# Token lists of a mixture-of-experts layer: half of them by scatters spread over the projections, half by one-hot products

## The chip, the cores and the metric

One core of a Trainium2 chip runs the whole kernel. The metric is the device time of one execution in microseconds (us), lower is better. TensorE (PE) multiplies matrices, VectorE (DVE) and ScalarE (ACT) work element by element, GpSimd (POOL) does some of that and issues all indirect DMAs, SyncE (SP) issues most loads. The engines run side by side, each through its own instructions in order, and wait for one another by semaphores.

## The reference

One decoder layer on 1024 tokens of width 1024, in float32: a mixer with one input and one output projection, a layer norm, a mixture of experts, and a second layer norm.

```python
proj = h @ w_in                       # 2560 columns: q, f, v, g of 4 heads, 4 pooling groups
...
h = layer_norm(ALPHA * h + mix @ w_out)
scores = sigmoid(h @ w_router)        # 64 experts
sel = scores + router_bias            # best 4 of 8 groups, then the best 8 experts in them
wts = scores[chosen] / sum * 2.5
for each expert e, for its tokens t:  # 256 hidden columns
    out[t] += wts[t, e] * (silu(h[t] @ w_gate[e]) * (h[t] @ w_up[e])) @ w_down[e]
out += shared expert on every token
return layer_norm(ALPHA * h + out)
```

Each token has 8 experts, so 8192 pairs of token and weight have to be sorted by expert before the experts can run: for each expert a list of its token numbers and a list of the weights. These lists are what the change is about.

## The kernel before, in words

The 1024 tokens are eight tiles of 128, in two halves. For each half the kernel projects x (20 projections of 128 columns, each 24 matmuls: 8 pieces of the contraction, three products each, since every operand is split into a high and a low float32r part), and after each projection it takes one to three pieces of the recurrent heads from the list `pend` (`for i, (kind, h) in enumerate(kinds[hf])`, line 854). Then `out_project(hf, ...)` does the output projection and layer norm. The one for the first half stands before the sixth projection of the second half (`OUT0_AT`).

At the end of an output projection two pairs of tiles are normed in turn, and `route(t0, pair)` is called for each pair (the second half's first pair somewhat later, among the matmuls of the next). It does four things. `choose` multiplies by the router's weights, takes the sigmoid (`scored[0]`) and finds the eight experts of a token; `mb` and `mk` are the 0/1 masks. `slots_of` counts with a triangular matrix on PE how many earlier tokens chose the same expert; that gives `code`, for each token and expert the row in a table in DRAM (`table`, 64 experts x 1152 slots x 2 numbers), and `c8`, the eight rows of each token. `send` works out the eight weights of each token on DVE (line 663) and issues, for each tile and each of its eight choices, an indirect DMA on POOL that writes 128 pairs of 8 bytes to these rows: 16 scatters for a pair of tiles, 64 in all (line 667). `preset` writes two tiles to the sums in DRAM.

After the last pair `rank_experts` sorts the experts by their load on PE and DVE (`perm` is the permutation matrix, `ids_i` the experts' numbers, by which the weights are loaded), and `send` issues the last 16 scatters. `rank_tables` reads 192 slots of each expert's list back through SP (line 737), makes three repeated copies on POOL (line 742) and turns the lists by matmuls with `perm` into `idx_a`, `idx_c`, `idx_s` and the gates: the row numbers by which POOL gathers tokens (line 904). It is called when the first routed unit is loaded, after the two units of the shared expert. Between the routing and the routed stage PE has the shared expert's work: four tiles held on the chip (`SharedHeld`, two groups: gate and up for all four, then down), and two units `Shared`. Then come 64 experts' units: gather, transposes, gate and up, down, scatter-add (line 1198), with the weights (3 MB for each expert) loaded by SP and split by ACT (line 71) and DVE (line 72).

The order of the instructions on each engine is made by a planner with cost estimates, which may move work as far as its data allow; `tc.issue_after(x)` ties instructions behind `x`. Only in the routed stage the order on PE is the one written. PSUM has four banks "pj", two "lv" and two "mi", taken in turn; a bank is taken again when its last reader is done.

Of the kernel before, what the change touches and what calls it, by code (L numbers as in the profile page):

```python
# [50 lines left out]
BEHIND = 3  # L51
IN_RANGE = "ids, counts and blocks are worked out on the chip within these bounds for any scores"
# [3 lines left out]
def tile_layer(ctx: ExitStack, tc: tile.TileContext, x, w_in, hg_lb_logits, hg_norm_g, w_pool, pool_scale, w_out,  # L56
# [385 lines left out]
    waiting = []  # L442
# [5 lines left out]
    def out_project(hf, mx, groups):  # L448

        hts = {}  # L450
        after = []
        for tiles, cols in groups:
            if cols[0] == 0:
                for t in tiles:
                    hts[t] = rows_tile()
                    r0 = (hf * NC4 + t) * P
                    nc.gpsimd.dma_start(hts[t], x[r0:r0 + P, :])
            pss = {(t, n): bank("pj") for t in tiles for n in cols}
            for i, k in enumerate(OUT_ORDER):
# [12 lines left out]
            if cols[-1] == 1:  # L472
                batches = [b for b in BATCHES[hf] if b[0] in tiles]
                for batch in batches:
                    pair = [hts[t] for t in batch]
                    layer_norm(rt, pair, lng, lnb, hf)
                    for t in batch:
                        nc.scalar.dma_start(h_ext[(hf * NC4 + t) * P:(hf * NC4 + t + 1) * P, :], hts[t])
                    go = lambda t0=hf * NC4 + batch[0], pair=pair: route(t0, pair)
                    if hf and tiles != groups[-1][0]:  # L480
                        after.append(go)
                    else:
                        chosen = go()
        return hf * NC4 + batches[-1][0], chosen

    def route(t0, pair):
        while waiting:
            with tc.issue_after(normed[0].ins):
                send(*waiting.pop())
        chosen = choose(t0, pair)  # L490
        if t0 + len(pair) < SEQ // P:
            waiting.append((t0, chosen, slots_of(t0, chosen)))
            if t0 < NC4:
                send(*waiting.pop())
        with tc.issue_after(scored[0].ins):
            preset(t0, pair)
        if t0 == NC4:
            shared_weights()
        return chosen
# [6 lines left out]
    def setup_dram(z):  # L506
        for i in range(DUMMY // P):
            nc.gpsimd.dma_start(h_ext[SEQ + i * P:SEQ + (i + 1) * P, :], z)
            nc.gpsimd.dma_start(acc[SEQ + i * P:SEQ + (i + 1) * P, :], z)
        pad = t2("k", 2).rearrange("p (s o) -> p s o", o=2)[:EXPERTS]  # L510
        nc.gpsimd.memset(pad, 0)
        nc.gpsimd.iota(pad[:, :, 0], pattern=[[1, DUMMY]], base=SEQ, channel_multiplier=0, allow_small_or_imprecise_dtypes=True)
        tv = table.rearrange("(e s) o -> e s o", s=SLOTS)
        for c in range(0, SLOTS, DUMMY):
            n = min(DUMMY, SLOTS - c)
            nc.gpsimd.dma_start(tv[:, c:c + n, :], pad[:, :n, :])
# [21 lines left out]
    def setup_router():  # L538
# [11 lines left out]
        nc.vector.tensor_scalar(tri, jp, 0.0, None, op0=ALU.is_gt)  # L550
        nc.vector.memset(onesb, 1.0)
# [4 lines left out]
    def rtile(tag, shape, dt=F32):  # L556
        if tag in places:
# [66 lines left out]
    def slots_of(t0, chosen):  # L624
# [25 lines left out]
        return code, c8, wt  # L650

    def send(t0, chosen, placed):

        hts = chosen[0]
        code, c8, wt = placed
        T = len(hts)
        pair = pairs[:, t0:t0 + T]
        scr = rtile("wscr", [EXPERTS])
        ci = slots[:, t0:t0 + T]
        placed_at[0] = nc.vector.tensor_scalar(ci, c8, -1.0, None, op0=ALU.add)  # L660
        for t in range(T):
            for j in range(8):
                nc.vector.scalar_tensor_tensor(scr[:, t, :], code[:, t, :], c8[:, t, j:j + 1], wt[:, t, :], op0=ALU.is_equal, op1=ALU.mult,
                                               accum_out=pair[:, t, j, 1:2])
        for t in range(T):
            for j in range(8):
                sc = nc.gpsimd.indirect_dma_start(out=table[:, :], out_offset=bass.IndirectOffsetOnAxis(ap=ci[:, t, j:j + 1], axis=0),
                                                  in_=pair[:, t, j, :], in_offset=None)
                for o in scatters:
                    tc.declare_no_dep(sc.ins, o.ins, reason="each token of an expert has a slot of its own")  # L670
                scatters.append(sc)
# [6 lines left out]

    ids_i = rc.tile([1, EXPERTS], I32, name="ids_i")
# [9 lines left out]
    def rank_experts(mb):  # L689
        E = EXPERTS  # L690
# [4 lines left out]
        for i, m in enumerate(parts):  # L695
            nc.tensor.matmul(pc[:E, E:E + 1], m, onesb[:, 0:1], start=i == 0, stop=m is parts[-1])
        cnt = rc.tile([P, 1], F32, name="cnt")
        nc.vector.tensor_copy(cnt[:E], pc[:E, E:E + 1])
        col = rc.tile([P, 2], F32, name="col")
        nc.gpsimd.iota(col[:, 0:1], pattern=[[0, 1]], base=0, channel_multiplier=1, allow_small_or_imprecise_dtypes=True)  # L700
        nc.vector.scalar_tensor_tensor(col[:E, 1:2], cnt[:E], float(E), col[:E, 0:1], op0=ALU.mult, op1=ALU.subtract)
# [3 lines left out]
        nc.vector.tensor_scalar(key[:E], key[:E], col[:E, 1:2], None, op0=ALU.is_gt, op1=ALU.add, accum_out=rank[:E])  # L705
        perm = rc.tile([P, E], F32, name="perm")
        nc.vector.tensor_scalar(perm[:E], iota_e[:E], rank[:E], None, op0=ALU.is_equal)
# [26 lines left out]
    def rank_tables(perm, tmp):  # L734
        E = EXPERTS
        lists = tmp[:, :384].rearrange("p (s o) -> p s o", o=2)
        nc.sync.dma_start(lists, table.rearrange("(e s) o -> e s o", s=SLOTS)[:, 0:192, :])
        p3 = bank("mi")
        nc.tensor.matmul(p3[:, 0:E], lists[:, 0:P, 0], perm[:E], start=True, stop=True)
        for i, n in enumerate((64, 32, 16)):  # L740
            same = tmp[:, 384 + i * P:512 + i * P]
            nc.gpsimd.tensor_copy(same.rearrange("p (m s) -> p m s", s=n), lists[:, None, P:P + n, 0].to_broadcast([E, P // n, n]))
            nc.tensor.matmul(p3[:, (1 + i) * E:(2 + i) * E], same, perm[:E], start=True, stop=True)
        for q in range(2):
            n = P if q == 0 else 64
            nc.tensor.matmul(p3[:n, (4 + q) * E:(5 + q) * E], lists[:, q * P:q * P + n, 1], perm[:E], start=True, stop=True)
        nc.vector.tensor_copy(idx_a, p3[:, 0:E])
# [14 lines left out]
        nc.vector.tensor_copy(gate_a, p3[:, 4 * E:5 * E])  # L762
        nc.vector.tensor_copy(gate_s, p3[0:64, 5 * E:5 * E + N_REST])
# [86 lines left out]
    for hf in range(2):  # L850
# [3 lines left out]
        for i, (kind, h) in enumerate(kinds[hf]):  # L854
            if hf == 1 and i == OUT0_AT:
                out_project(0, mx[0], GROUPS[0])
            if hf == 0 and i == 2:
# [4 lines left out]
            ps = project(kind, h, xT, lambda: pend and pend.pop(0)())  # L862
            if hf == 0 and i == 0:
# [18 lines left out]
    while pend:  # L882
        pend.pop(0)()
    left.close()
# [7 lines left out]
    t0, chosen = out_project(1, mx[1], GROUPS[1])  # L892
    right.close()
    cp = right.enter_context(tc.tile_pool(name="cp", bufs=1, side="right"))
    perm, counts = rank_experts(chosen[1])
    send(t0, chosen, slots_of(t0, chosen))
# [4 lines left out]
    lists = rt.tile([64, D], F32, tag="yc", name="yc", bufs=2)[:EXPERTS]  # L901
# [367 lines left out]
    def load_to(n):  # L1269
        while n_loaded[0] < min(n, len(units)):  # L1270
            if n_loaded[0] == n_shared:
                rank_tables(perm, lists)
# [100 lines left out]

    worst = load_i(nblk_i[0:1, EXPERTS:EXPERTS + 1], 0, MAX_BLOCKS, mybir.ALL_ENGINES)
    with tc.If(worst > 0):
        with tc.For_i(0, EXPERTS) as r:
# [71 lines left out]
```

## Time and profile before

| | |
|---|---|
| median of 3 runs | 1455.69 us (1450.94 to 1456.17) |
| the profiled execution | 1448.83 us |
| its span | 1447.1 us, mean granted PE clock 0.956 |
| busy | PE 91%, DVE 75%, ACT 60%, POOL 39% |
| DMA | 350 MB, mean 242 GB/s; 14480 packets under 512 B |

The span is the time from the first to the last instruction of the profiled execution. A busy share is that of the whole span; matmuls overlap in a pipeline, so a PE that is busy all the time need not be at its peak. The clock is that which the chip granted to PE, 1.00 for 2.4 GHz and 0.50 for 1.2 GHz. A releaser behind "<-" is what ended an engine's wait; "remote" is a signal that the profile can't put down to an instruction, and "issue" is a wait that nothing in the profile shows.

### The profile page before, as it was taken

What the parts mean: (1) busy time and instruction counts of PE and PEld (TensorE: products, weight loads), DVE (VectorE), ACT (ScalarE), POOL (GpSimd) and SP (SyncE); (2) the same over time, 40 slices, a digit from 0 to 9 for tenths busy, and PEclk for the clock granted to TensorE, in tenths of its full rate; (3) what the DMA queues carried; (4) which work ended last, traced back from release to release, by engine and by line L of the source; (5) the groups of instructions that cost most, each with busy time, mean ns of one, the idle gap of its engine ahead of it and who ended that gap; (6) DMA issues with size and microseconds to landing.
All of it is one profiled execution on the core that took longest, in us unless ns stands there. A gap on an engine that the chain in (4) does not pass through costs nothing. (4 is left out here: it accounts for less than half of the span.)

```text
span 1447.1 us, 21911 instructions
## 1 busy us (share of the span) xinstructions
PE 1323.3 (91%) x7055; PEld 1103.9 (76%) x7056; DVE 1087.4 (75%) x2168; ACT 871.6 (60%) x1625; POOL 558.3 (39%) x471
## 2 busy tenths in 40 slices
PE   8799999977998866999999899898999989999992
PEld 6688878866876655788877688787888877888871
DVE  6466864866777844777888688888889888888856
ACT  5233442332434221677777688777888877888855
POOL 3000000045012442454343455664656636565415
PEclk9899999997999988999999999999999999999996
DMA  7422243433125426999999899999999989999975
GB/s 236 153 59 66 59 126 92 134 108 73 51 74 181 140 61 201 327 352 337 322 355 349 258 364 328 319 361 336 323 365 353 344 292 330 360 352 351 365 201 219
DMA packets 138661, 350.07 MB, mean 242 GB/s; under 512 B 14480, under 2 KB 55520, under 8 KB 138544
## 3 DMA queue, kind: packets, MB, share of 16 engines
q1 hardware_dynamic: 110864, 258.08, 49.3%
q0 software_dynamic: 25664, 83.22, 22.1%
q10 hardware_dynamic: 2016, 7.34, 1.3%
q8 instruction: 56, 0.92, 0.2%
q14 instruction: 61, 0.50, 0.1%
HBM read 296.36 MB, written 52.23 MB: 241 GB/s over the span
## 5 line engine op out<-in xcount | busy, mean ns | idle before, releaser
L72 DVE TENSOR_TENSOR lo<-raw,hi 128x1024 fp32r<-128x1024 f32 (+1 forms) x490 | 485.4, 1024 | 62.6 <-ACT hi L71 50.3
L71 ACT ACTIVATE hi<-raw 128x1024 fp32r<-128x1024 f32 (+1 forms) x490 | 418.0, 888 | 49.5 <-DMA raw<-in_w_gate_dram 16.7
L1198 POOL DMA_INDIRECT acc<-ya,idx_a x64 | 149.4, 2334 | 289.7 <-ACT hi L71 77.5
L1159 PE MATMUL pj<-xt,hi 128*128 128x288 f32 (+3 forms) x768 | 205.8, 351 | 6.8 <-POOL xt L1145 4.8
L71 ACT ACTIVATE whi<-wraw 128x512 fp32r<-128x512 f32 x128 | 80.6, 630 | 205.6 <-PE pj L79 100.1
L1159 PE MATMUL pj<-xt,lo 128*128 128x144 f32 (+3 forms) x768 | 174.1, 237 | 0.0
L1159 PEld LDWEIGHTS pj<-xt,hi 128*128 128x128 f32 x768 | 150.5, 196 | 11.1 <-POOL xt L1145 5.3
L1159 PEld LDWEIGHTS pj<-xt,lo 128*128 128x128 f32 x768 | 149.8, 199 | 0.8
L78 PE MATMUL pj<-hi,xt 128*128 128x512 f32 x368 | 149.2, 406 | 0.8 <-DVE sg L1163 0.7
L79 PE MATMUL pj<-lo,xt 128*128 128x512 f32 x368 | 145.4, 395 | 0.0
L80 PE MATMUL pj<-hi,xt 128*128 128x512 f32 x368 | 145.0, 394 | 0.0
L72 DVE TENSOR_TENSOR wlo<-wraw,whi 128x512 fp32r<-128x512 f32 x112 | 76.6, 688 | 86.6 <-ACT whi L71 85.5
L78 PE MATMUL pj<-xh,whi 128*128 128x512 f32 x320 | 133.3, 417 | 2.0 <-ACT whi L71 2.0
L80 PE MATMUL pj<-xh,wlo 128*128 128x512 f32 x320 | 131.0, 410 | 0.0
L79 PE MATMUL pj<-xl,whi 128*128 128x512 f32 x320 | 130.1, 406 | 0.0
L78 PE MATMUL pj<-hi,hTh 128*128 128x512 f32 x240 | 98.1, 409 | 18.5 <-ACT hTh L71 15.9
L72 DVE TENSOR_TENSOR xt<-lv,xt 128x512 fp32r<-128x512 f32 x148 | 96.5, 682 | 11.5 <-ACT xt L71 10.8
L904 POOL DMA_INDIRECT h<-h_ext,idx_a x64 | 93.0, 1453 | 29.2 <-PE lv L916 11.4
L79 PE MATMUL pj<-lo,hTh 128*128 128x512 f32 x240 | 97.0, 404 | 0.0
L71 ACT ACTIVATE xt<-lv 128x512 fp32r<-128x512 f32 x148 | 81.7, 595 | 24.2 <-PE lv L916 15.3
L80 PE MATMUL pj<-hi,hTl 128*128 128x512 f32 x240 | 95.0, 402 | 0.0
L1193 POOL TENSOR_SCALAR yc<-yc,gate_s 16x1024 f32<-16x1024 f32 (+3 forms) x24 | 84.2, 3509 | 7.7 <-DVE yc L1192 7.7
(354 smaller groups left out, 2786.3 us busy)
## 6 DMA issues: line engine op xcount, KB each, us to landing
raw<-in_w_down_dram SPq DMA_DIRECT2D x128, 512.0 KB
raw<-in_w_gate_dram SPq DMA_DIRECT2D x127, 512.0 KB
raw<-in_w_up_dram SPq DMA_DIRECT2D x127, 512.0 KB
wraw<-in_w_in_dram SPq DMA_DIRECT2D x80, 256.0 KB
wraw<-in_w_out_dram SPq DMA_DIRECT2D x48, 256.0 KB
h<-in_x_dram POOLq DMA_DIRECT2D x8, 512.0 KB
h_ext<-h ACTq DMA_DIRECT2D x8, 512.0 KB
raw<-acc SPq DMA_DIRECT2D x8, 512.0 KB
```

The lines of the kernel that those rows point to most:

```text
L71: last_split[0] = nc.scalar.activation(hi, src, AF.Copy)
L72: (eng or nc.vector).tensor_sub(lo, src, hi.bitcast(F32))
L78: nc.tensor.matmul(ps, sh, mh, start=first, stop=False)
L79: nc.tensor.matmul(ps, sh, ml, start=False, stop=False)
L80: last_mm[0] = nc.tensor.matmul(ps, sl, mh, start=False, stop=last)
L904: nc.gpsimd.indirect_dma_start(out=g, out_offset=None, in_=h_ext[:, :], in_offset=bass.IndirectOffsetOnAxis(ap=idx, axis=0))
L1159: nc.tensor.matmul(ps[q][:, :cols], w, x[:, :cols], start=k + i == 0, stop=k + i == NK)
L1193: nc.gpsimd.tensor_scalar(rest[:cut], rest[:cut], gate_s[:cut, r:r + 1], None, op0=ALU.mult)
L1198: return nc.gpsimd.indirect_dma_start(out=acc[:, :], out_offset=bass.IndirectOffsetOnAxis(ap=idx, axis=0), in_=y, in_offset=None, compute_ ...
```

## The change

The first four tiles keep their scatters. Their routing is cut into steps that stand between the pieces of the heads in `pend`, and the 32 scatters become a list `drops`, of which three are issued after each projection, the first of the three behind the projection's last matmul. The last four tiles have no scatters. For each tile and choice, `list_up` makes a tile `sel` (for each token a row of 64 token numbers and 64 weights that is zero but at the chosen expert) and a tile `at` (for each token a row of 192 seats that is zero but at the token's seat), and adds `sel` transposed times `at` in one PSUM bank on PE: 128 rows (64 lists of numbers, 64 of weights) by 192 seats. The lists of the first half are read from the table into `kept`, and the sum of both is what `rank_tables` takes, now directly behind. Only 192 slots for each expert are cleared at the start; the whole table is filled and all 64 scatters are issued in a branch for experts with too many tokens, which is taken only for such scores.

```diff
+DROPS = 3
+LISTED = 192
...
+    def route_early(t0, pair):
+        got = []
+        def scores():
+            got.append(choose(t0, pair))
+            with tc.issue_after(scored[0].ins):
+                preset(t0, pair)
+        def places():
+            drops.extend(send(t0, slots_of(t0, got[0])))
+        return [scores, places]
...
+    def drop(n):
+        for i in range(min(n, len(drops))):
+            with tc.issue_after(last_mm[0].ins):
+                sc = drops.pop(0)()
+            if i == 0:
+                tc.add_manual_dep(sc.ins, last_mm[0].ins.name, ..., reason="a few at a time")
...
+    def list_up(t0, placed, ps, sels, first, last):
+        code, c8, wt, pos = placed
+        for t in range(2):
+            for j in range(8):
+                sel = sels[j % len(sels)]
+                at = cp.tile([P, LISTED], F32, tag="at", name="at", bufs=2)
+                gates(t0, placed, t, j, sel[:, 1])
+                nc.gpsimd.tensor_scalar(sel[:, 0], code[:, t, :], c8[:, t, j:j + 1], pairs[:, t0 + t, j, 0:1], op0=ALU.is_equal, op1=ALU.mult)
+                nc.vector.tensor_scalar(at, seats, pos[:, t, j:j + 1], None, op0=ALU.is_equal)
+                nc.tensor.matmul(ps, sel.rearrange("p a e -> p (a e)"), at, start=first and t + j == 0, stop=last and t + j == 8)
...
                 out_project(0, mx[0], GROUPS[0])
+                pend = [step for steps in itertools.zip_longest(routing, pend) for step in steps if step]
...
             ps = project(kind, h, xT, lambda: pend and pend.pop(0)())
+            drop(DROPS)
...
+    nc.gpsimd.iota(seats, pattern=[[1, LISTED]], base=SEQ, ...)
+    for q in range(2):
+        read = nc.gpsimd.dma_start(kept[q * EXPERTS:(q + 1) * EXPERTS], table.rearrange("(e s) o -> e s o", s=SLOTS)[:, 0:LISTED, :])
+        ...
+    listed = bank("pj")[:, :LISTED]
+    list_up(late[0][0], late[0][2], listed, sels, True, False)
+    perm, counts = rank_experts(late[1][1][1])
+    placed = slots_of(late[1][0], late[1][1])
+    ...
+    list_up(late[1][0], placed, listed, sels, False, True)
+    for q in range(2):
+        e = slice(q * EXPERTS, (q + 1) * EXPERTS)
+        nc.vector.tensor_add(lists[e], listed[e], kept[e, :, q])
+    rank_tables(perm)
```

`rank_tables` loses its read of the table; its three copies move from POOL to DVE. `rank_experts` counts on 128 partitions instead of 64.

## Rows read from the trace of the kernel before

**Rows 1.** Windows: engines' busy us (instructions), PE clock, DMA share, GB/s.

```profile
250.00:300.00 50.00, 50.00 (x252) 41.91 (x251) 39.18 (x104) 16.65 (x29) 1.06 (x2) 1.00 0.46 143
300.00:350.00 50.00, 36.36 (x175) 28.98 (x174) 27.40 (x161) 12.87 (x29) 33.76 (x33) 0.80 0.31 82
600.00:800.00 200.00, 200.00 (x957) 161.83 (x956) 163.18 (x210) 153.81 (x240) 87.16 (x41) 1.00 1.02 344
800.00:1400.00 600.00, 574.28 (x3382) 494.63 (x3381) 508.55 (x789) 483.92 (x935) 328.30 (x264) 0.97 0.99 333
```

**Rows 2.** The tile table: instructions, count, min/median/max ns, first and last start.

```profile
L667 POOL DMA_INDIRECT table<-pairs,slots x64: 953/963/2053, 305.0 to 552.5; - x64
L737 SPq DMA_DIRECT2D yc<-table x1: 562/562/562, 568.5 to 568.5; - x1
```

**Rows 3.** Windows: the stretches at the lower clock in the projections.

```profile
320.00:330.00 10.00, 4.01 (x18) 3.11 (x19) 3.94 (x26) 2.67 (x6) 6.43 (x8) 0.50 0.29 39
330.00:335.00 5.00, 5.00 (x23) 4.59 (x22) 5.00 (x34) 0.56 (x1) 3.91 (x4) 0.64 0.48 187
345.00:350.00 5.00, 4.87 (x12) 3.28 (x12) 1.58 (x7) 0.00 (x0) 4.00 (x4) 0.50 0.21 53
```

**Rows 4.** Timeline, POOL and ACT: start, us, instruction, idle before it, releaser.

```profile
304.96 1.10 POOL L667 DMA_INDIRECT table<-pairs,slots  x1 [16.95 <-DVE passing L663]
312.87 0.55 ACT L323 ACTIVATE sc<-lv 32x128 f32<-32x128 f32 x2 [4.64 <-remote]
329.95 1.02 POOL L667 DMA_INDIRECT table<-pairs,slots  x1 [2.35 <-DVE passing L663]
341.42 0.28 ACT L380 ACTIVATE w<-mi 128x128 f32<-128x128 f32 x1 [5.12 <-remote]
```

**Rows 5.** Windows: between the last output projection and the routed stage.

```profile
510.60:516.10 5.50, 0.37 (x2) 0.00 (x0) 0.00 (x0) 0.38 (x1) 4.28 (x5) 0.86 0.02 1
516.10:521.30 5.20, 5.17 (x15) 4.30 (x16) 0.00 (x0) 0.00 (x0) 3.00 (x4) 0.50 0.02 1
545.00:556.60 11.60, 0.14 (x2) 0.00 (x0) 2.38 (x7) 0.40 (x2) 6.68 (x7) 0.66 0.39 129
556.60:562.00 5.40, 5.36 (x13) 4.20 (x14) 2.15 (x4) 0.26 (x1) 0.00 (x0) 0.50 0.31 90
575.00:585.14 10.14, 8.64 (x45) 6.81 (x46) 8.08 (x21) 4.66 (x7) 7.53 (x7) 1.00 0.84 283
```

**Rows 6.** Timeline: the last routing and the lists, several engines.

```profile
515.69 0.38 ACT L585 ACTIVATE passing<-mi 128x256 f32<-128x256 f32 x1 [7.29 <-remote]
533.62 0.95 POOL L667 DMA_INDIRECT table<-pairs,slots  x1 [13.62 <-DVE passing L663]
552.55 0.96 POOL L667 DMA_INDIRECT table<-pairs,slots  x1 [0.30 <-issue]
556.21 0.66 ACT L71 ACTIVATE hTh<-mi 128x256 fp32r<-128x256 f32 x2 [11.99 <-remote]
577.86 0.23 DVE L747 CAST idx_a<-mi 128x64 int32<-128x64 f32 x1 [1.64 <-PE mi L746]
```

**Rows 7.** Durations: timeline once, then by line and shape: busy us, mean ns.

```profile
466.63 1.81 PE L579 MATMUL lv<-ident,h 128*128 128x128 f32 x8
L663 DVE SCALAR_TENSOR_TENSOR passing<-code,c,wt 128x64 f32<-128x64 f32 x32 | 7.0, 283 | 0.0
L72 POOL TENSOR_TENSOR wlo<-wraw,whi 128x512 fp32r<-128x512 f32 x16 | 21.6, 1359 | 109.4 <-ACT whi L71 94.6 <-DVE sc L327 14.7
L742 POOL COPY yc<-yc 64x128 f32<-64x128 f32 x3 | 1.7, 597 | 21.6 <-DMA raw<-in_w_down_dram 21.6
```

**Rows 8.** Timeline: a line of DVE beside POOL's work, and alone.

```profile
485.61 1.37 POOL L72 TENSOR_TENSOR wlo<-wraw,whi 128x512 fp32r<-128x512 f32 x1 [0.98 <-ACT whi L71]
486.22 0.80 DVE L609 TENSOR_SCALAR gr<-gr 128x16 f32<-128x16 f32 x1
526.05 0.17 DVE L609 TENSOR_SCALAR gr<-gr 128x16 f32<-128x16 f32 x1
```

More of the change, by code (lines that the diff above doesn't have):

```diff
@@ L478, in out_project, with route_late @@
                         nc.scalar.dma_start(h_ext[(hf * NC4 + t) * P:(hf * NC4 + t + 1) * P, :], hts[t])
-                    go = lambda t0=hf * NC4 + batch[0], pair=pair: route(t0, pair)
-                    if hf and tiles != groups[-1][0]:
-                        after.append(go)
-                    else:
[L483 to L489, printed above, removed]
-        chosen = choose(t0, pair)
[L491 to L496, printed above, removed]
+                    t0 = hf * NC4 + batch[0]
+                    if hf == 0:
+                        routing.extend(route_early(t0, pair))
+                    elif tiles != groups[-1][0]:
+                        after.append(lambda t0=t0, pair=pair: route_late(t0, pair))
+                    else:
+                        route_late(t0, pair)
+    routing = []
+    late = []
+    drops = []
+    def route_early(t0, pair):
[7 more added lines that the diff above has]
+        return [scores, places]
+    def route_late(t0, pair):
+        chosen = choose(t0, pair)
         if t0 == NC4:
+            late.append((t0, chosen, slots_of(t0, chosen)))
             shared_weights()
-        return chosen
+        else:
+            late.append((t0, chosen, None))
+    def drop(n):
[3 more added lines that the diff above has]
+            if i == 0:
+                tc.add_manual_dep(sc.ins, last_mm[0].ins.name, mybir.DependencyInfo(mybir.DependencyClass.Sync, mybir.DependencyReason.DATA), reason="a few at a time")
     h_ext = dram.tile([SEQ + DUMMY, D], F32, name="h_ext")
@@ L509, in setup_dram @@
             nc.gpsimd.dma_start(acc[SEQ + i * P:SEQ + (i + 1) * P, :], z)
[L510 to L516, printed above, removed]
+        nc.gpsimd.dma_start(table.rearrange("(e s) o -> e (s o)", s=SLOTS)[:, :2 * LISTED], z[:EXPERTS, :2 * LISTED])
     wr = rt.tile([P, NK * P], F32R, tag="xc", name="wr", bufs=2).rearrange("p (k e) -> p k e", k=NK)
@@ L556, in rtile @@
     def rtile(tag, shape, dt=F32):
+        if tag in ("gsc", "gr"):
+            c = places["lt"] + (0 if tag == "gsc" else 16)
+            return passing[:, c:c + 16].rearrange("p (t c) -> p t c", t=2)
         if tag in places:
@@ new lines, in slots_of, with gates @@
+        pos = rtile("pos", [8])
+        for t in range(T):
+            nc.vector.max(pos[:, t, :], base[:, t, :])
+        placed_at[0] = nc.vector.scalar_tensor_tensor(pos, c8, float(SEQ), pos, op0=ALU.add, op1=ALU.subtract)
+        return code, c8, wt, pos
+    def gates(t0, placed, t, j, out):
+        code, c8, wt, _ = placed
+        nc.vector.scalar_tensor_tensor(out, code[:, t, :], c8[:, t, j:j + 1], wt[:, t, :], op0=ALU.is_equal, op1=ALU.mult,
+                                       accum_out=pairs[:, t0 + t, j, 1:2])
@@ L658, in send @@
+    def send(t0, placed):
         scr = rtile("wscr", [EXPERTS])
-        ci = slots[:, t0:t0 + T]
-        placed_at[0] = nc.vector.tensor_scalar(ci, c8, -1.0, None, op0=ALU.add)
-        for t in range(T):
+        for t in range(2):
             for j in range(8):
-                nc.vector.scalar_tensor_tensor(scr[:, t, :], code[:, t, :], c8[:, t, j:j + 1], wt[:, t, :], op0=ALU.is_equal, op1=ALU.mult,
-                                               accum_out=pair[:, t, j, 1:2])
-        for t in range(T):
-            for j in range(8):
[L667 to L671, printed above, removed]
+                gates(t0, placed, t, j, scr[:, t, :])
+        return [lambda t=t, j=j: to_table(t, j) for t in range(t0, t0 + 2) for j in range(8)]
@@ new lines, in to_table @@
+    def to_table(t, j):
+        sc = nc.gpsimd.indirect_dma_start(out=table[:, :], out_offset=bass.IndirectOffsetOnAxis(ap=slots[:, t, j:j + 1], axis=0),
+                                          in_=pairs[:, t, j, :], in_offset=None)
+        for o in scatters:
+            tc.declare_no_dep(sc.ins, o.ins, reason="each token of an expert has a slot of its own")
+        scatters.append(sc)
+        return sc
+    def list_up(t0, placed, ps, sels, first, last):
+        code, c8, wt, pos = placed
+        for t in range(2):
+            for j in range(8):
+                sel = sels[j % len(sels)]
[4 more added lines that the diff above has]
+                nc.tensor.matmul(ps, sel.rearrange("p a e -> p (a e)"), at, start=first and t + j == 0, stop=last and t + j == 8)
@@ L694, in rank_experts @@
             nc.tensor.matmul(pc[:, 0:E], onesb, m, start=i == 0, stop=m is parts[-1])
[L695 to L701, printed above, removed]
+        for q in range(2):
+            for i, m in enumerate(parts):
+                nc.tensor.matmul(pc[q * E:(q + 1) * E, E:E + 1], m, onesb[:, 0:1], start=i == 0, stop=m is parts[-1])
+        nc.vector.tensor_copy(cnt, pc[:, E:E + 1])
+        nc.vector.scalar_tensor_tensor(col[:, 1:2], cnt, float(E), col[:, 0:1], op0=ALU.mult, op1=ALU.subtract)
         key = rc.tile([P, E], F32, name="key")
```

73 lines of the change are left out of this document (48 added, 25 removed).

## The prediction

> **What bounds the kernel now.** I read four views in this order. First the busy time by stretches: where does TensorE (PE) stand idle or run at the lower clock? From 600 to 800 us PE is busy for 200.00 of 200.00 us at clock 1.00 [rows 1]. That is the first quarter of the routed stage, so whatever makes that stage start earlier makes the kernel end earlier, as far as nothing else binds later. The projections of the first half run as well: 50.00 of 50.00 us between 250 and 300 [rows 1]. The stretch 300 to 350, which is the same kind of work, has 36.36 us and clock 0.80 [rows 1]. Something costs 13.6 us of idle time there, and a slow clock after it.
>
> Second, the view by tile of the table says what is different: 64 scatters of token lists on GpSimd (POOL), median 963 ns, the first at 305.0, the last at 552.5 [rows 2]. They come in four runs of 16, two in the projections, from 304.96 and 329.95 [rows 4], two after them. In a run one starts every 1.26 us: from 533.62 to 552.55 there are 15 steps [rows 6].
>
> Third, the timeline says how a scatter on POOL can stop PE. While a run lasts, signals between the other engines come late: ScalarE (ACT) waits 4.64 and 5.12 us, each ended by "remote", for results that PE has long issued [rows 4]. In the last run the wait is 11.99 us, and it ends at 556.21, under four microseconds after the last scatter started [rows 6]. So a scatter is not dear by itself; a long run of them is. The waits don't start with the run. The first run begins at 304.96, and the wait that ends at 312.87 began at 308.2, three scatters later; the second begins at 329.95, and the wait that ends at 341.42 began at 336.3, with its sixth scatter [rows 4]. I don't know the mechanism; I take the rows.
>
> Fourth, the end of the chain for the lists: they are read back at 568.5 [rows 2], behind the stores that the SP queue holds, and the indices for the first gather exist at 577.86 [rows 6].
>
> **The change part by part.** *Early scatters (the first four token tiles).* The same 32 scatters stay, in 11 groups of up to three after eleven projections. A group lasts 3 x 1.26 = 3.8 us; each group waits for the projection's last matmul, and behind that wait on POOL stand only the next scatters and the loads of x for the second output projection, which nothing wants before the projections are over. The routing steps are put between the head parts; from the loops I count that the list of head parts is as long at the end (5) as before, so nothing new is left over there. What the two runs cost now: idle 50 - 36.36 = 13.6 us; and work at the lower clock, 4.0 us of it between 320 and 330 at 0.50, 3.6 us between 330 and 335 (0.64 is 72% at 0.5), 4.9 us between 345 and 350 [rows 3], half of 12.5, or 6.2 us. Together 19.8 us. Ends of the gain: 19.8 if groups of three delay nothing, since no such wait began before the third scatter of its run; 0 if every scatter costs its 0.6 us wherever it stands; a loss is not excluded, one late signal per group, 11 x 0.5 us, or -5. I take 16, near the upper end, because the rows show the first three scatters of both runs free.
>
> *Late scatters (the last four tiles).* 32 scatters, the list read on SP and its landing go. What they cost on PE, by stretches [rows 5]: 510.6 to 516.1, idle 5.1; 516.1 to 521.3 at clock 0.50, 2.6 lost; 545 to 556.6, idle 11.5; 556.6 to 562 at 0.50, 2.7 lost; 575 to 585.1, idle 1.5 while lists and first gathers are waited for. Sum 23.4 us.
>
> *What is added on PE.* 32 matmuls in float32, 128 x 128 by 192 columns. Eight of 128 columns took 1.81 us [rows 7], 0.226 each; by columns 0.34, times 32 is 10.9 us. Ends: 7.2 us if a matmul costs no more than one of 128 columns, 21.7 us if all run at the lower clock.
>
> *What is added on VectorE (DVE) and POOL.* A step makes two one-hot tiles: a gate product on DVE (there before too, 0.28 us [rows 7]), a comparison of 128 x 192 on DVE (estimate 0.25 us, between 0.17 for one input of 16 columns with POOL idle [rows 8] and the 0.28) and a product on POOL of 128 x 64, between 0.597 us for a copy of 64 x 128 and 1.36 us for 128 x 512 with two inputs [rows 7]; I take 0.6. Do DVE and POOL overlap? The rows say not always: while POOL worked from 485.61 for 1.37 us, a DVE operation on 16 columns, issued at 486.22, took 0.80 us and ended with it; the same line took 0.17 us with POOL idle [rows 8]. So I let a step take the sum, 0.6 + 0.28 + 0.25 = 1.13 us, instead of 0.6. For the last pair of tiles that is 16 x 1.13 = 18.1 us where 16 scatters took 16 x 1.26 = 20.2.
>
> The Trainium skill ("SBUF — State Buffer", § SBUF: two separate sides) says that VectorE and GpSimd hold one port pair exclusively, for a whole instruction, when VectorE runs in a two-port mode or reads two inputs from SBUF. The trace agrees in the 0.80 us above. By that rule the 18.1 us stand, without it the list would be 9.6 us; it speaks against this change, since it moves a step of the lists from the DMA to exactly this pair.
>
> *When the lists are ready.* The last pair's scores waited 7.29 us for a late signal at 515.69 [rows 6]. Without scatters I put the start of the last pair's lists 7 us earlier, at 526.5 instead of 533.6. Then 18.1 for the steps and some 3 for ranking give indices at about 547.6, 30 us earlier than now. PE then has the shared expert's work for the last four tiles to do, so most of these 30 us are not on its path. One thing is: the product sums in one of the four PSUM banks "pj" from its first to its last step, and the fourth of the held tiles wants that bank. I charge 2 us of waiting (0 to 12). The experts' weights can be loaded once the ranking names them, and move with it.
>
> Late gain: 23.4 - 10.9 - 2 = 10.5 us; ends -10 (list matmuls at the lower clock and 12 us of waiting) and 23 (all of the added matmuls in holes that PE has anyway).
>
> *At nothing:* five table fills at the start become one (POOL, beside the first projections); ranking on 128 instead of 64 partitions, three more matmuls of one column; three copies that move from POOL to DVE; two table reads on POOL instead of one on SP (0.56 us [rows 2]), which wait for scatters of the projections. If their cover failed they would cost a microsecond or two. The filling of the table for the overflow case stands in a branch that isn't taken.
>
> **Sum.** 16 + 10.5 = 26.5 us. Against the profiled execution, 1448.8 us, that is 1422.3; the median of the runs shown, 1455.7, lies 6.9 us above it, so the forecast for a median is 1429. About 0.5%, or 7 us, is what a measurement of this kernel can tell from no change.
>
> **The rivals.** *A. A scatter costs what it costs, in groups or not.* For it: each group still has 3.8 us of POOL, and a projection lasts hardly longer. Against: the rows on the first scatters of a run. Early gain 0, late 10.5: 1445.
>
> *B. The lists cost PE as much as the scatters did.* The steps come every 1.13 us, the matmul takes 0.34, and the bank is held; if PE stands behind them for the 12.5 us left of the late part, only the early 16 remain: 1440.
>
> *C. The start of the routed stage isn't what binds.* From 800 to 1400 PE is busy for 574 of 600 us and the DMA share is 0.99 [rows 1]. If the weights' stream set the end, and it can't run before the shared expert's buffers are free, most of the gain would be given back: some 5 us are left, 1451.
>
> *D. Slower.* PE works in its written order. If the 32 list matmuls stand there ahead of the shared expert's work, PE waits in each step for POOL and DVE. With POOL's upper end, 1.36, DVE's 0.53 and 0.3 for handing over a step is 2.2 us, and PE waits 1.9 in each, 60 us in all. With half of them hidden behind other work the late part comes to 12.5 - 30 = -17.5 us, with the early 16 to 1457; with none hidden to 1487; middle 1472. It decides from 0.9 us of waiting a step (32 x 0.9 is 28.5 us, the early 16 and the late 12.5). Against it: 0.6 us is nearer to a one-input operation on 64 columns, and the order is made by a planner that sees the waits.
>
> **How the numbers follow.** Forecast with both gains, 1408 to 1440: 0.56. A 0.11, B 0.14, C 0.10, D 0.09. The range 1406 to 1452 leaves out D and the tails of the forecast and C. Faster by over 0.5% (below 1448.4) are the forecast, B and nearly all of A: 0.80. Within 0.5% C and a little of A and D: 0.12. Slower: 0.08.
>
> **What would show it.** In the profile after: no wait over 3 us ended by "remote" between 300 and 420, and a clock of 1.00 there (early step); scatters in eleven groups, none after 420; no scatter between 490 and 560; 32 matmuls of 192 columns near 0.34 us each, POOL's operations in the list near 0.6; indices before 555 and the full stretch of PE beginning some 25 us earlier. The prediction is wrong if groups of three delay signals as long runs did, if PE waits more than 12 us among the list's matmuls, or if the routed stage takes longer than before by what it started earlier.

## The result, and the profile after

| | before | after |
|---|---|---|
| median of 4 runs | 1455.9 us (1450.9 to 1459.2) | 1437.7 us (1435.8 to 1440.9) |
| the profiled execution | 1448.8 us, span 1447.1 | 1436.5 us, span 1434.7 |

The ratio is 0.988, 95% interval 0.9845 to 0.9915: 18.2 us by medians, where 26.5 were forecast. Only a part of it came by the steps of the forecast.

Windows of the kernel after (columns as in [rows 1]):

```profile
300.00:350.00 50.00, 33.45 (x163) 26.89 (x162) 31.38 (x164) 15.94 (x35) 31.95 (x31) 0.83 0.35 90
475.00:500.00 25.00, 13.54 (x61) 10.71 (x60) 21.75 (x73) 2.43 (x4) 10.78 (x13) 0.73 0.28 102
500.00:600.00 100.00, 97.94 (x478) 78.09 (x477) 70.91 (x242) 37.14 (x61) 40.32 (x39) 1.00 0.67 215
```

The last line is the step that worked: PE is full from 500 on, where before had the holes of [rows 5]. The first is the step that did not: PE is as empty as in [rows 1] (36.36 there). The second is a new hole. The timeline of POOL after shows why the first hole is still there:

```profile
300.54 1.10 POOL L698 DMA_INDIRECT table<-pairs,slots  x1 [15.46 <-DVE passing L686]
...
318.69 1.91 POOL L698 DMA_INDIRECT table<-pairs,slots  x1 [0.30 <-issue]
...
325.75 1.03 POOL L698 DMA_INDIRECT table<-pairs,slots  x1 [3.98 <-DVE passing L686]
...
342.20 0.97 POOL L698 DMA_INDIRECT table<-pairs,slots  x1 [0.30 <-issue]
346.14 1.21 POOL L698 DMA_INDIRECT table<-pairs,slots  x1 [2.97 <-PE pj L82]
358.05 0.97 POOL L698 DMA_INDIRECT table<-pairs,slots  x1 [10.70 <-PE pj L82]
```

No groups of three: 15 scatters in a row, then 13, then four single ones. Only the first scatter of a group waits for a matmul. The other two are tied to nothing: by its definition `tc.issue_after(x)` orders only instructions of x's own engine, `last_mm` is one of PE's, and the scatters are POOL's. So the planner was free to move those of the last groups ahead. For the first 15 the awaited matmuls were over when the slots existed. So late signals (waits ended by "remote") are there as in [rows 4] (waits by line: us in all, times, longest):

```profile
ACT whi L73 <- remote: 8.5, 2, 4.6
DVE k L333 <- remote: 6.6, 1, 6.6
ACT sc L325 <- remote: 6.4, 1, 6.4
```

The new hole, in PE's timeline, is the last pair's layer norm, with nothing for PE to do beside it:

```profile
483.51 0.39 PE L82 MATMUL pj<-whi,mxl 128*128 128x512 f32 x1
492.42 1.90 PE L601 MATMUL lv<-ident,h 128*128 128x128 f32 x6 [8.52 <-DVE h L442]
```

The last pair's lists on POOL, and the indices that answer to the last line of [rows 6]:

```profile
515.07 0.92 POOL L713 TENSOR_SCALAR made<-code,c,pairs 128x64 f32<-128x64 f32 x1 [4.94 <-DVE c L668]
...
521.41 1.94 POOL L713 TENSOR_SCALAR made<-code,c,pairs 128x64 f32<-128x64 f32 x1
...
530.29 0.67 POOL L713 TENSOR_SCALAR passing<-code,c,pairs 128x64 f32<-128x64 f32 x1
...
532.70 0.22 DVE L784 CAST idx_a<-mi 128x64 int32<-128x64 f32 x1
```

To see where the time went I took from each trace the starts of all PE matmuls of 128x512 into "pj" (3504, in the same order outside the stretch between the last output projection and the shared expert's end) and subtracted them one by one. A column is such a matmul; its heading is its start in the kernel before. Positive: the first-named kernel is ahead.

```
us of lead at               52    284    368    481    610   1004    end
after against before       3.4    4.1    6.4    8.7   15.3   21.4   12.4
```

So 3.4 us come at the start, 0.7 up to 284, 4.6 in the projections (284 to 481), 6.6 between output projection and routed stage (481 to 610), and 2.9 are lost later. The profiled execution of before is 7.1 us below its median, that of after 1.2 below; hence 12.4 here and 18.2 by medians.

### The profile page after: what moved, and what is told of

Its sections match the earlier page's. It is cut to its first block, busy times and chain, and to the rows that moved or that the text cites. A ratio compares the mean times of both kernels' runs of the same rounds, so it can differ in the third digit from the quotient of the medians.

```text
span 1434.7 us, 22119 instructions
## 1 busy us (share of the span) xinstructions
PE 1325.5 (92%) x7122; PEld 1105.2 (77%) x7123; DVE 1096.0 (76%) x2218; ACT 871.8 (61%) x1625; POOL 552.2 (38%) x465
## 4 chain that ended last, share of the span: by engine, by line
PE 63%; DVE 12%; DMA 11%; ACT 5%; issue 4%; POOL 2%; another core or an unknown queue 1%; SPq 0%; POOLq 0%; ACTq 0%; DVEq 0%
PE pj L80 13%; PE pj L81 13%; PE pj L82 13%; PE pj L1229 7%; DMA raw<-in_w_up_dram 6%; DVE lo L74 4%; PE lv L986 3%; PE lv L321 3%; ACT hi L73 2%; PE pj L1259 2%; DMA acc<-ya,idx_a 1%; PE pj L1165 1%; PE pj L1166 1%; PE pj L1188 1%
## 5 line engine op out<-in xcount | busy, mean ns | idle before, releaser
L1268 POOL DMA_INDIRECT acc<-ya,idx_a x64 | 134.6, 2103 | 271.0 <-ACT hi L73 102.9
L974 POOL DMA_INDIRECT h<-h_ext,idx_a x64 | 105.0, 1640 | 50.2 <-DVE hTl L74 14.5
L1263 POOL TENSOR_SCALAR yc<-yc,gate_s 16x1024 f32<-16x1024 f32 (+3 forms) x24 | 88.3, 3678 | 8.6 <-DVE yc L1262 8.6
```

Source lines behind the costliest of these rows:

```text
L974: nc.gpsimd.indirect_dma_start(out=g, out_offset=None, in_=h_ext[:, :], in_offset=bass.IndirectOffsetOnAxis(ap=idx, axis=0))
L1263: nc.gpsimd.tensor_scalar(rest[:cut], rest[:cut], gate_s[:cut, r:r + 1], None, op0=ALU.mult)
L1268: return nc.gpsimd.indirect_dma_start(out=acc[:, :], out_offset=bass.IndirectOffsetOnAxis(ap=idx, axis=0), in_=y, in_offset=None, compute_ ...
```

## The experiments

They fell on four chips, and the kernel before, run beside them on each, showed that this mattered more than any edit. I call the chip of the first pair A and the others B to E. The record doesn't say which chip A was; it behaves like B and may be the same one. Each ratio is to the kernel before on the same chip.

**Four edits on chip C** (kernel before there: 1405.8 us, not 1455.9).

*Groups that stand apart.*

```diff
 def drop(n):
+    aged[0] += bool(drops)
+    if aged[0] <= 3: return
     ...
-            if i == 0:
+            if True:
                 tc.add_manual_dep(sc.ins, last_mm[0].ins.name, ...)
```

> The changed kernel, but the scatters really stand in eleven groups: all three of a group wait for the last matmul of their projection (in the changed kernel only the first does), and the first group stands three projections later, so that PE has not passed the awaited matmul long before the slots exist. Theory 1: long runs of scatters delay signals and groups of three do not. Then no wait over 3 us ended by 'remote' is left between 300 and 420 us, PE is idle there for under 4 us instead of 16.6 in 300 to 350, and the time falls from 1437.7 to about 1421 (1417 to 1427). Rival A of the prediction: a scatter costs what it costs wherever it stands; then the idle time is spread over 300 to 420 and the time stays at 1435 to 1440.

Measured: 1423.3 us, ratio 1.012 (1.008 to 1.016), slower than before. The first two groups still run together, six scatters from 300.38 on; from the third group on they stand apart (POOL):

```profile
308.53 2.05 POOL L703 DMA_INDIRECT table<-pairs,slots  x1 [0.30 <-DVE u L397]
310.58 1.16 POOL L458 DMA_DIRECT2D h<-in_x_dram  x2
317.61 1.50 POOL L703 DMA_INDIRECT table<-pairs,slots  x1 [5.86 <-PE pj L82]
319.42 1.01 POOL L703 DMA_INDIRECT table<-pairs,slots  x1 [0.30 <-DVE S L357]
320.73 0.97 POOL L703 DMA_INDIRECT table<-pairs,slots  x1 [0.30 <-issue]
323.81 1.58 POOL L703 DMA_INDIRECT table<-pairs,slots  x1 [2.12 <-PE pj L82]
```

No wait ended by "remote" is left in the whole trace, but the next kernel shows that this says nothing about groups.

*Late part alone.*

```diff
-                        routing.extend(route_early(t0, pair))
+                        for step in route_early(t0, pair):
+                            step()
+                        while drops:
+                            drops.pop(0)()
```

> The late part of the change alone: the first four tiles are routed and scattered right behind their output projection, 16 scatters in a run, as in the kernel before; the last four keep their lists by one-hot products, and the single fill of the table stays. Theory: the early edit did little, since its scatters still ran in runs of 15 and 13; by the lead that the changed kernel gains in the projections (4.1 us at 274 us, 8.7 us at 384 us) this costs about 4.6 us: 1442 (1439 to 1446). Rival: the early edit brought its 16 us and the lists little: 1452 to 1456.

Measured: 1425.7 us, ratio 1.013 (1.009 to 1.017). Its scatters run back to back as in the kernel before, and yet the window 300 to 350 is full:

```profile
300.00:350.00 50.00, 49.93 (x289) 40.86 (x288) 45.45 (x204) 23.74 (x50) 35.23 (x34) 1.00 0.42 107
```

On this chip a run of scatters delays nothing. Neither theory of these two expectations could be tested there.

*Five fills of the table.*

```diff
-        nc.gpsimd.dma_start(table...[:, :2 * LISTED], z[:EXPERTS, :2 * LISTED])
+        tv = table.rearrange("(e s) o -> e (s o)", s=SLOTS)
+        for c in range(0, 2 * SLOTS, 2 * DUMMY):
+            n = min(2 * DUMMY, 2 * SLOTS - c)
+            nc.gpsimd.dma_start(tv[:, c:c + n], z[:EXPERTS, :n])
```

> The changed kernel with the whole table cleared at the start, in five DMAs as before (with zeros) instead of one of 192 slots for each expert. Theory: the 3.8 us of lead that the changed kernel has from 52 us on come from the fills, behind which the first heads' parameters arrive late: 1441.5 (1440 to 1444), the wait of PE for DVE's k near 45 us 7.4 us as before instead of 4.7. Rival, the prediction's own term: the fills are hidden, and something else made the lead: 1437.7, wait 4.7 us.

Measured: 1424.2 us, ratio 1.014 (1.009 to 1.018), the same as its neighbours. PE's only wait of note near 45 us, with five fills and then in the late part alone with one:

```profile
PE lv L321 <- DVE k L333: 5.9, 1, 5.9
```

```profile
PE lv L321 <- DVE k L333: 4.5, 1, 4.5
```

In all kernels with one fill it is 4.1 to 5.4, so the fills explain 0.5 to 1.8 of the start's 3.4 us, and perhaps less: in the table of leads below this kernel (3.0 at 53 us) lies among those with one fill (1.9 to 4.4). The other edit there is the memory that was filled from, a tile "k" that the heads' own k also takes turns in. The four profiles with five fills from "k" (the kernel before on A, B and D, and the early part alone) have a wait of 6.7 to 7.8 us, so that this tile is worth 0.8 to 1.9.

*List matmuls twice.*

```diff
-                nc.vector.tensor_scalar(at, seats, pos[...], None, op0=ALU.is_equal)
-                nc.tensor.matmul(ps, sel, at, ...)
+                nc.vector.tensor_scalar(at, seats, pos[...], 0.5, op0=ALU.is_equal, op1=ALU.mult)
+                for m in range(2):
+                    nc.tensor.matmul(ps, sel, at, ...)
```

> The changed kernel with each of the 32 list matmuls issued twice (with seats of 0.5, so that the sums are the same). Theory: from 500 us on PE is full, so each added matmul is on the path with its start-to-start time, 0.2 to 0.34 us: 32 of them 6 to 11 us, 1444 to 1449. Rival C: what starts later in the routed stage is made up there; then under 3 us, 1438 to 1440. Rival D: the product waits for POOL and DVE in each step and PE has room there: 0 to 3 us and a hole between 495 and 512.

Measured: 1434.9 us, ratio 1.019 (1.015 to 1.024), 10.6 us over the kernel with five fills (a sixth execution took 7318 us; why is open, and it is left out). The table below finds it between output projection and shared expert: 26.5 us lost there, against 16.2 as the mean of the five kernels with the list in the same bank. So 32 matmuls cost 10.3 us, 0.32 each, and all of it is on the path. Rivals C and D fall for this term.

**Is it the chip? Chip B.** *The kernel before once more.*

> The kernel before once more, on the chip of this call. In the four runs of the last call the kernel before took 1405.8 us where it had taken 1455.9, and the first four tiles' scatters, still 13 to 32 in a row, had no wait ended by 'remote' beside them. Theory 2: the late signals belong to the chip (or its state) of the first pair of runs, not to the scatters alone; then the kernel before has no such wait here either, PE is busy for over 48 of 50 us between 300 and 350 and the late part (500 to 600) over 90 of 100 instead of 74. Rival: the kernel before has them here as well and is faster for another reason (the weights' stream).

Measured: 1453.3 us (the 17 runs of before on this chip: median 1456.1), with late signals again, the longest wait 9.7 us:

```profile
300.00:350.00 50.00, 36.48 (x177) 29.15 (x175) 28.80 (x163) 13.30 (x30) 32.58 (x33) 0.83 0.33 86
500.00:600.00 100.00, 75.44 (x334) 60.11 (x335) 52.55 (x177) 29.65 (x49) 43.56 (x42) 0.86 0.54 177
```

So the forecast of no such wait here missed, and so did the rival, since the kernel isn't faster. That is nothing against theory 2: to test it the kernel before has to be read on a chip where it is fast, and chip D has that.

*Early part alone*: the kernel before with `route_early`, `drop` and the interleaved `pend` of the change, all else as it was.

> The kernel before with the early part of the change alone (routing in steps between the heads' pieces, three scatters after each projection); late scatters, table fills and read as before. Theory 2 on a chip without late signals: nothing to gain, within 5 us of the kernel before. If the chip has them: 4 to 5 us faster than before.

Measured: 1451.1 us, ratio 0.996 (0.993 to 0.999): about 5 us. It fits the 4 to 5 us expected for a chip with late signals. Its first 32 scatters bunch as in the kernel after (15, 13, four single), PE is busy for 32.50 of 50 us from 300 to 350. In its profile it is 2.9 us behind before at the end of the projections; a gain of 5 by medians and that don't agree, and I leave it at "little".

*The kernel after once more.*

> The changed kernel once more, beside the kernel before on one chip. Theory 2: where the kernel before has no late signals the change is slower, by the 16 to 20 us that its three variants of the last call were (ratio 1.012 to 1.014): about 10 us for 32 list matmuls and the rest for lists that are ready later than by scatters. If the chip has late signals: faster by 12 to 22 us (ratio 0.985 to 0.991).

Measured: 1444.7 us, ratio 0.992 (0.988 to 0.995): faster, as on chip A, by 11.4 us, a little less than expected.

**Chip D.** *Groups of three again*, and *groups of eight, eight, four, four, four, four* (`sizes = [8, 8, 4, 4, 4, 4]`, one for each projection).

> The changed kernel with all three scatters of a group tied to the end of their projection (eleven groups, three projections later), on another chip. If the chip delays signals during runs of scatters: theory 1 (only long runs delay) has no 'remote' wait over 3 us in 300 to 420, PE busy for over 46 of 50 us in 300 to 350 instead of 33, and a ratio to the kernel before of 0.974 to 0.984 where the changed kernel had 0.988 and 0.992. Rival A (each scatter costs its 0.5 to 0.6 us): the idle time is spread, PE busy 60 to 62 of the 75 us in 350 to 425, ratio 0.988 to 0.994. If the chip does not delay signals: ratio 1.010 to 1.016 as in the run of this kernel before.

> The same, but the first 16 scatters in two groups of eight and the other 16 in four groups of four. If the chip delays signals: theory 1 in its form 'from the third or fourth scatter on' has 'remote' waits of 2 to 6 us beside the two groups of eight and under 2 us beside the groups of four; if only runs of more than ten delay, none beside either; rival A has about 4.5 us of PE's idle time for each group of eight and 2.2 for each of four. If the chip does not delay: no 'remote' wait, time within 5 us of the run with groups of three.

Measured: 1423.4 us, ratio 1.012 (1.009 to 1.016), and 1418.3 us, ratio 1.010 (1.006 to 1.013). The second edit made no such groups: its 32 scatters start from 300.65 to 345.16, with POOL idle for at most 0.31 us between two of them, so they are two runs of 16 again, with the loads of x between. There are no late signals on this chip either, so neither kernel tells what a group's size does where there are some.

> The kernel before, for a profile on the chip of this call. If the chip delays signals: PE busy for 36 us between 300 and 350 and 74 between 500 and 600, as in both profiles so far, 1450 to 1466 us. If not: over 48 of 50 and over 90 of 100, 1400 to 1416 us, and the routed stage begins earlier than in the changed kernel's variants on such a chip.

Measured: 1397.0 us (the 11 runs of before on this chip: median 1405.5). This is the kernel before where nothing is delayed, to be laid beside [rows 1] and [rows 5]:

```profile
300.00:350.00 50.00, 50.00 (x290) 41.18 (x289) 45.82 (x211) 22.80 (x47) 34.98 (x34) 1.00 0.45 108
475.00:500.00 25.00, 22.23 (x125) 17.75 (x125) 19.33 (x134) 7.29 (x15) 18.48 (x20) 1.00 0.27 62
500.00:600.00 100.00, 93.40 (x436) 76.96 (x435) 70.63 (x116) 55.09 (x87) 48.91 (x35) 0.97 0.98 320
```

The scatters themselves last as long as on chip A ([rows 2]: median 963 ns):

```profile
L667 POOL DMA_INDIRECT table<-pairs,slots x64: 954/967/2055, 304.9 to 515.2; - x64
```

**The hole at 483, chip E** (before: 1403.0 us). *The list in another bank*, and *that with groups that stand apart*.

```diff
-    listed = bank("pj")[:, :LISTED]
+    listed = bank("lv")[:, :LISTED]
```

> The changed kernel with one word changed: the lists' product sums in a bank of 'lv' instead of 'pj'. Theory 3: the prediction's term '2 us of waiting for the pj bank' was too small; with that bank held, the shared expert's matmuls can't stand ahead of the last pair's transposes, and PE is empty for 8.5 to 9.7 us while the last layer norm runs. Then that wait (PE for DVE's h) is under 2 us here, PE is busy for over 20 of 25 us between 475 and 500, and the ratio to the kernel before falls by about 0.007 (10 us): to 0.980 to 0.986 on a chip with late signals, to 1.002 to 1.007 on one without. Rival: the lists are the longer chain, and what PE does early it waits for later: ratio as of the changed kernel, 0.988 to 0.992 or 1.010 to 1.014.

> Both edits: the list in a bank of 'lv' and the early scatters in eleven groups that really stand apart. On a chip with late signals, theory 1 (only long runs delay): no 'remote' wait over 3 us in 300 to 420, PE busy for over 46 of 50 us in 300 to 350 instead of 33, and 10 to 16 us less than the run with the list's bank alone: ratio 0.970 to 0.978. Rival A (each scatter costs what it costs): within 4 us of the run with the bank alone. On a chip without late signals: within 4 us of it, as there runs of 16 cost nothing.

Measured: 1421.8 us, ratio 1.014 (1.010 to 1.019), and 1418.5 us, ratio 1.013 (1.008 to 1.018). The hole is gone. PE's longest wait from 420 to 545, of the late part alone (list in "pj", chip C), then of the list in "lv":

```profile
PE lv L604 <- DVE h L442: 9.7, 1, 9.7
```

```profile
PE lv L388 <- DVE w L385: 3.5, 1, 3.5
```

And the window 425 to 475 of the two, in the same order:

```profile
425.00:475.00 50.00, 34.36 (x156) 27.12 (x155) 44.00 (x100) 18.15 (x27) 17.47 (x15) 0.88 0.53 177
```

```profile
425.00:475.00 50.00, 43.25 (x183) 34.67 (x184) 42.94 (x101) 19.26 (x29) 13.47 (x10) 0.86 0.55 183
```

The planner now puts some 42 of the shared expert's matmuls where PE was empty. The whole time did not follow: 1.014 and 1.013 lie in the rival's range, 1.010 to 1.014, and not in theory 3's, 1.002 to 1.007. Their intervals are over 10 us wide, so by ratios this is no gain that can be told, and one of 7 us isn't ruled out either. By stages it is one (next table, 457 to 563), and it is still there at 953; at the end one of the two kernels is no further ahead than the kernel with groups of three. The rival, that PE waits later for what it did early, has no row for it in that stage; what is lost in the routed stage differs as much between other kernels.

```
lead in us over the kernel before on chip D (its starts in the heading)
                             53    284    343    457    563    953    end
before on chip A            0.5    0.0  -24.9  -24.8  -47.4  -51.9  -51.9
groups of three (C)         3.9    4.8   -0.2    1.2  -15.3  -12.6  -24.3
groups of three (D)         1.9    2.4   -2.7   -1.3  -16.3  -18.0  -27.5
late part alone (C)         1.9    2.3    2.0    1.5  -14.9  -17.7  -28.0
five fills (C)              3.0    4.2   -0.9    3.6  -12.8  -11.5  -22.7
list matmuls twice (C)      3.2    3.4   -5.6   -3.8  -30.3  -25.7  -37.9
groups of 8 and 4 (D)       4.4    4.6   -0.5    2.9  -13.7  -12.2  -15.9
list in lv (E)              3.5    3.5   -5.4   -3.3  -11.8  -10.8  -24.2
list in lv, groups (E)      3.7    4.1   -0.9    1.9   -7.9   -6.3  -16.2

lead in us over the kernel before on chip B (columns as for chip A above)
                             51    282    364    478    606    999    end
after (B)                   1.8    1.3    0.1    1.5    7.4    8.5   12.6
early part alone (B)       -1.5   -2.5   -6.4   -5.4   -9.5   -3.5    0.3
```

The profile of before on chip D lies 8.4 us below its median there, so its last column makes the others look worse than their medians do.

The two blocks price every part. Up to 284 us, where no scatter has run, the kernel before is equally fast on A and D (0.0); then it is 24.8 us behind on A in the projections and 22.6 more behind them (first line). I take this as the price of the late signals, since the losses fall where the scatters and the waits stand; another difference of the chips in the same stretches isn't ruled out. The late part, on chips without late signals, costs 16.5, 15.0, 16.4, 16.4 and 16.6 us (457 to 563, five kernels), mean 16.2, and with the list in "lv" 8.5 and 9.8, mean 9.2. On a chip with late signals it should then bring 22.6 - 16.2 = 6.4 us; the two profiles of the kernel after have 6.6 and 5.9.

No version that I ran beats the kernel before on both kinds of chip. The changed kernel itself did not run on a chip without late signals; seven variants of it did, on three chips, and all were slower than before there, by 1.0 to 1.9%. The last variant did not run on a chip with late signals, where by the sums above it should bring the most. That groups of three escape the delays was the core of the early step, and is still open.

## Why the prediction was right or wrong, by its steps

The forecast, 1429 in 1406 to 1452, was right in sign and held in its range, 8.7 us off by medians, though its largest term failed. That is in part luck: the result lies nearest to the figure of rival B (1440), by which the early 16 us come and the late part brings nothing, and what came is the reverse, little early and something late; and a start for which nothing was forecast makes up for 4.1 us. Against the profiled execution it was 1422.3, and that took 1436.5. The 14.2 us between are, by the leads: early part 11.4 less than forecast (4.6 for 16), late part 3.9 less (6.6 for 10.5), 2.9 lost in the routed stage, and 4.1 gained before 284 us where nothing was forecast.

- *Late signals, and their size: right.* I counted 19.8 + 23.4 = 43.2 us that runs of scatters cost now; the same kernel on a chip without them is 24.8 + 22.6 = 47.4 us ahead at the shared expert. The early term was low by 5. One row I read wrongly: ACT waited 4.64 us to 312.87 [rows 4], but PE began the awaited matmuls only at 310.31, so the signal was at most 2.6 us late, and the idle time before a "remote" is no measure of that. The 11.99 us to 556.21 [rows 6] are nearly all real: the awaited matmuls ended at 544.91, 11.3 us before:

```profile
310.31 1.00 PE L319 MATMUL lv<-qp,k 128*128 128x64 f32 x8
544.28 0.63 PE L956 MATMUL mi<-ident,hh 128*128 128x128 f32 x4
```

- *"Each group waits for the projection's last matmul": wrong, and the largest miss.* Only the first scatter of a group waits, and the awaited matmul may be long over. The early gain was 4.6 us on chip A and 0.2 on chip B, for 16. The wait stands in the diff for `i == 0` alone, and nothing held the others; that could have been read. Routing in steps between the heads' pieces may cost something itself: the seven kernels with it lose 0.6 to 7.2 us between 284 and 457 where nothing is delayed, the one without it 0.8. All seven have this wait of PE between 300 and 312, which neither that one nor the kernel before on D has:

```profile
PE pj L82 <- DVE wlo L74: 1.9, 1, 1.9
```

- *List matmuls, 10.9 us: right, by luck.* It was 10.3, by doubling them. But the eight matmuls of [rows 7] from which I worked it out ran at a clock of 0.53. From 466.63 to PE's next matmul at 468.09 they took 0.18 each; four of the same, at 1.00, took 0.09 each. And the profile has each list matmul as two, 64 for 32. Twice the price for half the number cancel, and the upper end of 21.7 us at the lower clock rests on the same slip (windows and timeline of before, then the tile table of after):

```profile
466.63:468.09 1.46, 1.46 (x10) 1.46 (x8) 1.46 (x2) 0.47 (x1) 0.00 (x0) 0.53 1.03 295
471.32:471.67 0.35, 0.35 (x5) 0.35 (x4) 0.02 (x1) 0.00 (x0) 0.35 (x1) 1.00 0.79 269
471.32 0.60 PE L579 MATMUL lv<-ident,h 128*128 128x128 f32 x4
L715 PE MATMUL pj<-at,made x32: 324/326/690, 494.5 to 530.6; 128*128 128x192 f32 x32
L715 PE MATMUL pj<-at,passing x32: 323/326/527, 495.2 to 531.3; 128*128 128x192 f32 x32
```

- *"2 us for the pj bank": mis-sized.* It cost 16.2 - 9.2 = 7.0 us in this stage; that the whole time is shorter without it isn't shown. I saw the bank as something that the fourth held tile waits for. What the traces show is that with the list in "pj" the shared expert's matmuls stand behind the last layer norm, and with the list in "lv" 42 of them ahead of it; that the planner gave the list the next free bank first is my reading.
- *Late gain 10.5: it was 6.6 and 5.9*, since 22.6 - 10.3 - 7.0 is 5.3, within 1.3 of both.
- *List step 1.13 us: 1.0.* 16 steps took from 515.07 to 530.96. The first eight took 0.79 each (515.07 to 521.41), less than the 1.3 of POOL's 0.73 in these steps (for 0.6) and DVE's 0.28 and 0.32 one after the other. So the sum that I took from [rows 8] doesn't hold for a whole step. Two single steps took 1.94 and 2.28, each beside a DVE operation of 1.21 us with two inputs:

```profile
521.10 1.21 DVE L74 TENSOR_TENSOR lo<-ya,hi 128x1024 fp32r<-128x1024 f32 x1
524.83 2.28 POOL L713 TENSOR_SCALAR passing<-code,c,pairs 128x64 f32<-128x64 f32 x1
525.17 1.21 DVE L74 TENSOR_TENSOR lo<-ya,hi 128x1024 fp32r<-128x1024 f32 x1
```

  By the Trainium skill ("SBUF — State Buffer", § SBUF: two separate sides) a DVE operation with two inputs and a POOL operation share one port pair, and the one that has it blocks the other for its whole length. The first long step agrees with that, since the DVE operation had begun before it. In the second POOL's began first and DVE's was no longer for it, so these rows don't settle it; and the steps of 0.79 us don't show the two engines taking turns throughout.
- *Indices at 547.6: they came at 532.70*, 45 us earlier than in [rows 6], and it was worth little. On chips without delays they exist at 516.0 (groups of three, chip C) against 529.6 in the kernel before, and the routed stage still starts 15 us later. So there it isn't the lists that set the start.
- *"At nothing": wrong for the start*, 3.4 us on chip A and 1.8 on chip B came at the start, where I had called everything hidden.
- *Rival C: a little.* Between 610 and the end the kernel after loses 2.9 us on chip A and gains 5.2 on chip B; so by these two profiles the start of the routed stage binds, within some 5 us.
- *The rivals B and D on PE's waits* fall: ahead of the list matmuls PE is idle for 2.2 us in all in chip A's profile (0.6 for the one of the two buffers, 1.6 for the other).

## What to carry to other kernels

A cost that the trace shows as a wait for a late signal may belong to the chip it was taken on: run the kernel before on a second one ahead of any work on it. To space instructions in time every one of them needs a wait, on something that isn't over yet; an order given to the planner doesn't do that, and `issue_after` on another engine's instruction gives not even an order. Before a matmul's price is taken from a row, look up the clock in that stretch and how many records one matmul makes. And a PSUM bank held through a long sum is priced, in its stage, by what the other takers of that bank could have done in the meantime, not by the sum's own length.

## What the runs showed of the hardware

On chips A and B (one chip, perhaps), during runs of 13 to 16 indirect scatters of 128 x 8 bytes, signals between other engines came late: by at least 11.3 us in one case on A, where the wait for it was 11.99 us ([rows 6]; the longest such wait in the kernel before on B is 9.7). On chips C, D and E the same scatters, as long on POOL (median 967 ns on D) and as close together, delayed nothing: none of the nine traces has a wait ended by "remote", and the same kernel took 1403 to 1406 us instead of 1456. Why the chips differ I could not find out: the profiles of A and B have no time to landing for any DMA, so that those of the scatters can't be compared; on D the kernel before has 4.0 us in the median. Whether it is the chip, its state or how it is set up is open.
